# Layer 2's values and 12 of its 16 gates made ahead of its attention by seven block products for eight, by way of DRAM

## The chip, the cores and the metric

One core of one Trainium2 chip runs the kernel. The metric is the device time of one launch in microseconds (us), where a lower number is better. Five engines work beside each other, each through its own instructions in order: TensorE (PE in the profile; its weight loads are PEld), VectorE (DVE), ScalarE (ACT), GpSimd (POOL), and SyncE (SP), which issues all of this kernel's DMA transfers.

## The reference, cut to what matters

One step of a two-layer encoder over T = 576 tokens (512 of a prompt, 64 of a running stream), model width 2048. Layer 1 mixes stick-breaking attention and a state-space branch, projects, and ends in a layer norm. Layer 2 is what the change touches:

```python
def odd_layer(x, past_k, past_v, w_in, rel_bias, w_out, ln_g, ln_b):
    proj = jnp.einsum('bld,de->ble', x, w_in)          # 2048 -> 4 * 2048
    q, k, v, g = jnp.split(proj, 4, axis=-1)           # 32 heads of 64
    o = chunk_band_attention(q, k, v, past_k, past_v, rel_bias) * jax.nn.silu(g)
    mix = jnp.einsum('ble,ed->bld', o, w_out)
    return layer_norm(DEEPNORM_ALPHA * x + mix, ln_g, ln_b)
```

All is float32. The keys and values of layer 2 are outputs too.

## The kernel before

Activations lie feature-major: a feature tile is 128 features (partitions) by 576 tokens, and the model has 16 of them. Every float32 operand is split into a high and a low part of the type fp32r (`split`, L79: ACT makes the high part at L84, DVE the low part at L85), and each product of tiles is three matmuls: high weights with high data, high with low, low with high. `product` (L100) makes one output tile: two weight tiles of 128 x 1024 are fetched (`fetch`, L88, SP) and split, and then 16 feature tiles x 3 terms x 2 halves of 288 tokens = 96 matmuls run into one PSUM tile `pj` of two (`terms`, L115; the matmul is L123). The two halves follow each other on the same weights, except with `seq=True`, where the whole first half of the tokens goes ahead of the second. Raw weight tiles have two buffers, their split parts three.

Layer 1 ends in `mix_norm` (L633): the output projection, then, with no product left that could run, the normalisation tile by tile (POOL L741, DVE L742, ACT L746 and L748, DVE L749), which leaves the split activations `yh`, `yl` in SBUF and the sum of them in DRAM (`y_scr`, L751). The first two products of layer 2 (`first`, L761: the queries and the keys of head pair 0) run over the tokens as these come.

Layer 2 then goes over 16 head pairs (`run_pairs`, L505). For a pair `heads_in` (L420) makes queries, keys and values, three products, and turns the values token-major; then comes the pair's gate, a fourth product with its SiLU (`silu`, L126: four ACT and two DVE operations); then `ca_attend` (L780): logits, softmax, transposes and the weighted sum of values, gated in `place` (L527) and stored to `o_scr1`. The last four pairs leave their gate for after the loop (`ndefer` = 4), so that products run beneath the end of the last attention. The output projection and layer norm (`mix_norm`, L847) read `o_scr1` back.

Nothing here sets the order of the engines' instructions by hand: a scheduler with its own model of times takes the operations of all stages and lays them out on each engine, so products stand between the attention's small matmuls. Each engine then runs its own list in that order. So what the diff writes in one place may stand in several on the engines, and rows of that order are shown with the change.

Of the kernel before, what the change touches and what calls it, by code (L numbers as in the profile page):

```python
# [46 lines left out]
def encoder(ctx: ExitStack, tc: tile.TileContext, a):  # L47
# [78 lines left out]
    def silu(pl, src, dst, n, tag):  # L126
        """dst = src * sigmoid(src), sigmoid through exp(min(x, 0) - log(1 + exp(-|x|)))."""
        t = pl.tile([P, 580], F32, tag=tag, name=tag, bufs=2)[:, :n]
# [5 lines left out]
        tt(dst, src, t, ALU.mult)  # L134
# [38 lines left out]
    # ------------------------------------------------------------------ SSD branch  # L173
# [72 lines left out]
    SMP = 515               # column of the first sample token in a conv output  # L246
    for g in range(NG):
# [3 lines left out]
        # token-major x * dt, x * to_end, and B  # L251
# [9 lines left out]
        # masked (C B^T)^T  # L261
# [10 lines left out]
        # states  # L272
# [29 lines left out]
        # sample tokens of the whole group  # L302
# [26 lines left out]
        for i in range(4):  # L329
# [4 lines left out]
            # y of two heads  # L334
# [60 lines left out]
    def qk_sample(dst, qb, kh, kl):  # L395
        """dst [128 (2 heads x 64 queries), keys] = q . k from the block-diagonal parts of q."""
# [17 lines left out]
    def back(ap):  # L414
        """The view with its last free dim reversed."""
# [4 lines left out]
    def heads_in(pe, pl, w, mq, mk, mv, okd, ovd, pr, tiles, flipq=False, ready=None):  # L420
# [4 lines left out]
        pq = ready[0] if ready else product(w, mq, 2, xh, xl)  # L425
# [10 lines left out]
        pk = ready[1] if ready else product(w, mk, 2, xh, xl)  # L436
# [31 lines left out]
    def transpose_tile(wsrc, r, t, wts, flipq=False):  # L468
        """wsrc [128 queries of tile t of head r, keys] -> wts[block][:, head, queries of t]."""
# [26 lines left out]
    def sample_pv(blocks):  # L496
        """blocks: (w^T [keys, 128 (2 heads x 64 queries)], v [keys, 128]) -> PSUM [128, 64 queries]."""
# [29 lines left out]
    def place(pl, gt, po, get_sample, flipq=False):  # L527
        """Gated (or raw) head-pair output, feature-major [128, T]."""
# [14 lines left out]
    # ------------------------------------------------------------------ stick-breaking heads  # L543
# [411 lines left out]
```

## Time and profile before

| what | value |
|---|---|
| median of 3 runs (lowest to highest) | 2737.45 us (2735.05 to 2740.14) |
| span of the profiled execution | 2731.6 us |
| what lies between that span and the median | 5.85 us |
| instructions | 47,350 |
| PE busy | 2680.1 us, 98% |
| DVE busy | 1530.9 us, 56% |
| ACT busy | 1155.0 us, 42% |
| DMA, mean over the span | 110 GB/s |

The profile is of one execution. No time other than its span is recorded for that execution itself; the median of the runs stands in for it, 5.85 us above the span. Busy shares are averages over stages that differ, so the stages have to be read apart. Matmuls overlap in the pipeline, so a matmul's own duration (about 0.3 us) is not what it costs: the distance from the start of one to the start of the next is.

### The profile page before, as it was taken

Reading aid. Unit: us, or ns where it says so; the run is one execution under the profiler, and the core shown is the slowest. Engines: PE = TensorE matmul, PEld = TensorE weight load, DVE = VectorE, ACT = ScalarE, POOL = GpSimd, SP = SyncE. Lnnn points to the kernel's source line nnn. Section 1 sums busy time; section 2 is a strip of 40 time slices with the busy share of each in tenths; the row PEclk is TensorE's granted clock in tenths of the full one; section 3 lists DMA queues with packets and bytes.
Section 4 is the critical chain, followed back from the end, with each engine's and each line's share of the span. In section 5 each row is a group of like instructions: output and inputs, shape, how many; then the busy total and the mean of one; then the engine's idle time right before and its main releaser. Section 6 shows DMA issues by size and latency. Waiting matters only on the chain.

```text
span 2731.6 us, 47350 instructions
## 1 busy us (share of the span) xinstructions
PE 2680.1 (98%) x20126; PEld 2577.3 (94%) x20126; DVE 1530.9 (56%) x2328; ACT 1155.0 (42%) x1938; POOL 94.1 (3%) x172
## 2 busy tenths in 40 slices
PE   9999999999999999999998999999999999999996
PEld 8999899999999999999998999999999999999995
DVE  6665657665656767653338545444445555554437
ACT  5434344434555656541225434333334343344224
POOL 0000000000000000000004000000000000000004
PEclk9999999999999999999999999999999999999998
DMA  5222222223232222353235433333333333334334
GB/s 188 78 84 85 66 95 68 93 79 107 91 103 99 92 93 83 109 189 99 95 111 173 142 104 116 110 110 114 114 109 115 109 113 118 114 111 156 104 103 140
DMA packets 111060, 299.33 MB, mean 110 GB/s; under 512 B 12672, under 2 KB 26752, under 8 KB 110848
## 3 DMA queue, kind: packets, MB, share of 16 engines
q1 hardware_dynamic: 110848, 296.30, 32.8%
q8 instruction: 158, 2.59, 0.4%
q14 instruction: 54, 0.44, 0.0%
HBM read 250.82 MB, written 45.42 MB: 108 GB/s over the span
## 4 chain that ended last, share of the span: by engine, by line
PE 95%; DVE 3%; ACT 1%; issue 0%; DMA 0%; SPq 0%; ACTq 0%; DVEq 0%
PE pj L123 79%; PE po L493 3%; PE tpw L473 2%; PE px L123 2%; DVE d L742 1%; PE z L393 1%; PE z L392 1%; PE pos L502 1%; PE z L398 1%; PE pst L287 1%; PE py L356 1%; PE py L358 0%; PE tpw L485 0%; PE tpv L452 0%; PE pcb L338 0%
## 5 line engine op out<-in xcount | busy, mean ns | idle before, releaser
L85 DVE TENSOR_TENSOR wl<-raw,wh 128x1024 fp32r<-128x1024 f32 x367 | 450.6, 1228 | 490.3 <-ACT wh L84 488.3
L84 ACT ACTIVATE wh<-raw 128x1024 fp32r<-128x1024 f32 x367 | 388.3, 1058 | 739.7 <-PE pj L123 632.9
L123 PE MATMUL pj<-yl,wh 128*128 128x288 f32 x2048 | 464.4, 300 | 6.8 <-DVE yl L749 6.8
L123 PE MATMUL pj<-yh,wl 128*128 128x288 f32 x2048 | 455.2, 299 | 0.0
L123 PE MATMUL pj<-yh,wh 128*128 128x288 f32 x2048 | 451.8, 298 | 1.1 <-DVE kf L438 0.9
L123 PEld LDWEIGHTS pj<-yl,wh 128*128 128x128 f32 x2048 | 336.2, 189 | 10.8 <-DVE yl L749 9.0
L123 PEld LDWEIGHTS pj<-yh,wl 128*128 128x128 f32 x2048 | 333.3, 189 | 13.7 <-issue 12.2
L123 PEld LDWEIGHTS pj<-yh,wh 128*128 128x128 f32 x2048 | 336.0, 189 | 5.1 <-issue 2.0
L123 PE MATMUL pj<-oh,wl 128*128 128x288 f32 (+2 forms) x1120 | 254.7, 297 | 3.2 <-DVE wl L85 3.2
L123 PE MATMUL pj<-ol,wh 128*128 128x288 f32 (+2 forms) x1120 | 254.9, 297 | 0.0
L123 PE MATMUL pj<-oh,wh 128*128 128x288 f32 (+2 forms) x1120 | 254.3, 297 | 0.0
L123 PEld LDWEIGHTS pj<-oh,wl 128*128 128x128 f32 x1120 | 186.3, 189 | 3.9 <-DVE wl L85 3.4
L123 PEld LDWEIGHTS pj<-oh,wh 128*128 128x128 f32 x1120 | 186.1, 189 | 0.5
L123 PEld LDWEIGHTS pj<-ol,wh 128*128 128x128 f32 x1120 | 185.8, 189 | 0.3
L741 POOL TENSOR_TENSOR d<-d,mu 128x288 f32<-128x288 f32 (+2 forms) x60 | 60.2, 1038 | 1996.4 <-DVE mu L727 1211.3
L808 ACT ACTIVATE t<-t,smx 128x128 f32<-128x128 f32 (+3 forms) x128 | 71.1, 556 | 83.0 <-DVE smx L806 53.7
L466 ACT ACTIVATE wts<-tpw 128x128 f32<-128x128 f32 (+1 forms) x96 | 41.5, 432 | 127.2 <-PE tpw L473 127.0
L833 DVE TENSOR_TENSOR t<-z,bp 128x128 f32<-128x128 f32 (+3 forms) x128 | 60.5, 485 | 49.8 <-PE tpw L473 46.0
L493 PE MATMUL po<-wts,vt 128*64 128x384 f32 (+3 forms) x384 | 82.6, 442 | 0.0
L464 DVE COPY wts<-tpw 128x128 f32<-128x128 f32 (+1 forms) x96 | 46.7, 487 | 49.7 <-PE tpw L473 48.7
L676 DVE TENSOR_TENSOR d<-xr,pj 128x576 f32<-128x576 f32 (+3 forms) x30 | 20.2, 672 | 88.3 <-PE pj L123 88.3
L453 ACT ACTIVATE vt<-tpv 128x512 f32<-128x512 f32 x24 | 14.2, 594 | 126.4 <-PE tpv L452 126.4
(433 smaller groups left out, 5509.2 us busy)
## 6 DMA issues: line engine op xcount, KB each, us to landing
raw<-w_in SPq DMA_DIRECT2D x272, 512.0 KB, 3.3
raw<-w_out SPq DMA_DIRECT2D x95, 512.0 KB, 3.2
xr<-xT SPq DMA_DIRECT2D x29, 288.0 KB, 5.9
o_scr<-of SPq DMA_DIRECT2D x24, 288.0 KB, 3.0
d<-o_scr SPq DMA_DIRECT2D x24, 288.0 KB, 5.8
o_scr<-z SPq DMA_DIRECT2D x16, 288.0 KB, 2.2
or<-o_scr SPq DMA_DIRECT2D x16, 288.0 KB, 3.3
y_scr<-d SPq DMA_DIRECT2D x16, 288.0 KB, 3.9
```

The lines of the kernel that those rows point to most:

```text
L84: act(hi, src, AF.Copy)
L85: tt(lo, src, hi.bitcast(F32), ALU.subtract)
L123: mm(ps[:, at.start + v.start:at.start + v.stop], st[:, c], mv[u * 8 + k][:, v], start=(first and k == 0 and i == 0), stop=(last and k == ...
L287: mm(pst, btok[0:n, c, :], xe[0:n], start=True, stop=True)
L356: mm(o, xdt[:, c, hc], w4[:, r, c, :], start=True, stop=(c == 0))
L464: nc.vector.tensor_copy(dst, src)
L466: act(dst, src, AF.Copy)
L473: nc.tensor.transpose(tp[:, b * P:(b + 1) * P], wsrc[:, b * P:(b + 1) * P], ident)
L493: mm(po[q, b * P:TP], vt[:, b, q], wts[:, b, r, b * P:TP], start=(b == 0), stop=(b == 3))
L741: (tt if tail and m in (0, 1, 2, 3) else nc.gpsimd.tensor_tensor)(r, r, mu[:, v], ALU.subtract)
L808: act(t[:, i, :], t[:, i, :], AF.Exp, bias=sm[:, i:i + 1], accum_out=sm[:, 2 + i:3 + i])
L833: tt(tv[:, i, :], z[:, i * n:i * n + n], bp[seg[i][0]][:, TP - n:TP], ALU.add)
```

## The change

For two output tiles at once, one of the values and one of the gates (the last time two of the values), the 16 feature tiles are taken as two blocks of 8, the 576 tokens as two halves and the two outputs as two rows: a 2 x 2 by 2 x 2 block product. It is made by Strassen's scheme in Winograd's form, with seven block products of 8 feature tiles x 3 terms = 24 matmuls of 288 tokens (`seven`, L163; the matmul is L179), where two plain products take eight. It needs sums of weight blocks, four DVE operations of 128 x 1024 for each seven (L192, L195, L200, L203), and sums of blocks of the activations, made once (`sums_of`, L144): `y_scr` is loaded back in pairs of feature tiles, DVE makes four sums of 288 tokens of each pair (L152 to L155), and two tiles of sums are split (`ta`, `tb`). Results leave PSUM by four ACT copies and three DVE additions per seven.

Ahead of the attention there are now: two plain products with `seq=True` for the values of pairs 14 and 15 (`first`, L844), and 13 sevens, 12 for value and gate of pairs 0 to 11 and one for the values of pairs 12 and 13. Values go to a new DRAM tile `v_scr` and to the output `o_cav`, gates after their SiLU to `g_scr`. The attention loads both (L522, L592) where it had made them. Queries, keys, and the four last gates stay plain products. The pools of the sevens use the memory that `mix_norm` had before and the attention has behind them.

```diff
+    def sums_of(pl, tmp, src):
+        b12, b14 = [], []
+        for k in range(8):
+            ya, yb = (tmp.tile([P, T], F32, tag="so", name="so", bufs=4) for _ in range(2))
+            load(ya, src[k])
+            load(yb, src[8 + k])
+            tt(ya[:, 0:HALF], ya[:, HALF:T], ya[:, 0:HALF], ALU.subtract)
+            tt(ya[:, HALF:T], yb[:, HALF:T], ya[:, HALF:T], ALU.subtract)
+            tt(yb[:, HALF:T], yb[:, HALF:T], ya[:, 0:HALF], ALU.subtract)
+            tt(yb[:, 0:HALF], yb[:, 0:HALF], yb[:, HALF:T], ALU.subtract)
+            b12.append(split(pl, ya, [P, T], f"ta{k}"))
+            b14.append(split(pl, yb, [P, T], f"tb{k}"))
...
+    def seven(w, m0, m1, sums, ps, tmp):
...
+            for k in range(8):
+                c = slice(k * P, (k + 1) * P)
+                hi, lo = b[k]
+                for i, (st, mv) in enumerate(((wh, hi), (wh, lo), (wl, hi))):
+                    mm(acc, st[:, c], mv[:, v], start=(first and k == 0 and i == 0),
+                       stop=(k == 7 and i == 2), skip_group_check=not first)
+
+        a11, a21, a22 = raw(m0, 0, "sr", tmp, 4), raw(m1, 0, "sr", tmp, 4), raw(m1, 1, "sr", tmp, 4)
+        s_ = raw(None, 0, "raw", wpool, 2)
+        a12 = raw(m0, 1, "raw", wpool, 2)
...
+        mul(pa, "M1", a11, True)
+        act(c11, pa, AF.Copy)
+        tt(s_, a21, a22, ALU.add)
+        mul(pc, "M5", s_, True)
+        act(c22, pc, AF.Copy)
+        tt(s_, s_, a11, ALU.subtract)
+        mul(pa, "M6", s_, False)
+        act(c12, pa, AF.Copy)
+        mul(pb, "M2", a12, True)
+        tt(c11, c11, pb, ALU.add)
+        tt(a21, a11, a21, ALU.subtract)
+        mul(pa, "M7", a21, False)
+        tt(c22, c22, pa, ALU.add)
+        tt(s_, a12, s_, ALU.subtract)
+        mul(pc, "M3", s_, False)
+        tt(c12, c12, pc, ALU.add)
+        mul(pa, "M4", a22, False)
+        act(c21, pa, AF.Copy)
...
-        pv = product(w, mv, 2, xh, xl)
         vf = pe.tile([P, T], F32, tag="kvf", name="vf", bufs=2)
-        nc.vector.tensor_copy(vf, pv)
-        store(ovd[pr], vf)
+        if mv is None:
+            load(vf, ovd[pr])
...
-                pg = product(wg, gate0 + pr, 2, xh, xl)
                 gt = lt.tile([P, T], F32, tag="gt", name="gt", bufs=1)
-                silu(lt, pg, gt, T, "st")
+                if gates is None:
+                    silu(lt, product(wg, gate0 + pr, 2, xh, xl), gt, T, "st")
+                else:
+                    load(gt, gates[pr])
...
-    first = [product(a["w_in1"], m, 2, xh, xl, seq=True) for m in (0, 16)]
+    NSEV = 12
+    ps7 = pool("ps7", bufs=1, space=PSUM)
+    first = [product(a["w_in1"], 32 + m, 2, xh, xl, seq=True) for m in (14, 15)]
+    tp7 = pool("t7", bufs=1, side="left")
+    tm7 = pool("tm7", bufs=1, side="left")
+    for m, pv in zip((14, 15), first):
+        vf = tm7.tile([P, T], F32, tag="so", name="so", bufs=4)
+        nc.vector.tensor_copy(vf, pv)
+        store(v_scr[m], vf)
+        store(a["o_cav"][m], vf)
+    sums = sums_of(tp7, tm7, y_scr)
+    for i in range(NSEV + 1):
+        pair = (i, i) if i < NSEV else (12, 13)
+        o0, o1 = seven(a["w_in1"], 32 + pair[0], (48 if i < NSEV else 32) + pair[1], sums, ps7, tm7)
+        store(v_scr[pair[0]], o0)
+        store(a["o_cav"][pair[0]], o0)
+        if i < NSEV:
+            silu(tm7, o1, o1, T, "st7", 1)
+            store(g_scr[i], o1)
+        else:
+            store(v_scr[pair[1]], o1)
+            store(a["o_cav"][pair[1]], o1)
```

**Where the first products of layer 2 end, on PE.** Before, the second sequential product (its last rows read `yh15`) was followed by the next product of the attention (`pj_15394`), whose data all lie in SBUF:

```order
L123 MATMUL pj_15232<-yh15_14926,wl_15242 128x288
...
L123 MATMUL pj_15394<-yh0_14911,wh_15397 128x288 x2
L123 MATMUL pj_15394<-yl0_14927,wh_15397 128x288 x2
L123 MATMUL pj_15394<-yh0_14911,wl_15398 128x288 x2
```

Now the first seven stands there: M1 into `pa`, one matmul of M5 on the first sum `ta0h`, then M2 (`pb`), then the rest of M5 and M6 on the sums of each k in turn:

```order
L125 MATMUL pj_15237<-yh15_14928,wl_15247 128x288
L179 MATMUL pa_15497<-yh0_14913,wh_15502 128x288
...
L179 MATMUL pb_15498<-yl8_14937,wh_15591 128x288
L179 MATMUL pc_15499<-ta0h_15368,wh_15532 128x288
L179 MATMUL pb_15498<-yh8_14921,wl_15592 128x288
...
L179 MATMUL pb_15498<-yh15_14928,wl_15592 128x288
L179 MATMUL pc_15499<-ta0l_15369,wh_15532 128x288
...
L179 MATMUL pc_15499<-ta7h_15480,wl_15533 128x288
L179 MATMUL pa_15497<-tb7h_15484,wh_15562 128x288
...
L179 MATMUL pc_15499<-yh8_14921,wh_15651 128x288
```

So PE comes to data that are made at that moment; M3 (the last row), M7 and M4 stand behind all of the sums.

**The same place on DVE and SP.** DVE's list, behind the last `yl` of the layer norm (L829 in the new numbering): copies of the plain values, the sums, and the low parts and sums of weights, in one row:

```order
L829 TENSOR_TENSOR yl_14944<-d,yh_14928 128x288
L849 COPY so<-pj 128x576
L87 TENSOR_TENSOR wl<-sr,wh 128x1024
L192 TENSOR_TENSOR raw<-sr 128x1024
L200 TENSOR_TENSOR sr<-sr 128x1024
L849 COPY so<-pj 128x576
L87 TENSOR_TENSOR wl<-raw,wh 128x1024
L152 TENSOR_TENSOR so<-so 128x288
L195 TENSOR_TENSOR raw<-raw,sr 128x1024
...
L87 TENSOR_TENSOR wl<-raw,wh 128x1024 x2
L87 TENSOR_TENSOR ta0l<-so,ta0h 128x576
L203 TENSOR_TENSOR raw<-raw 128x1024
```

SP's list at that place, the loads of weights, stores and loads of `y_scr` behind its last stores:

```order
L831 DMA y_scr<-d 128x2x288 x8
L168 DMA sr<-w_in 128x1024 x4
L850 DMA v_scr<-so 128x576
L851 DMA o_cav<-so 128x576
L150 DMA so<-y_scr 128x576
L151 DMA so<-y_scr 128x576
L150 DMA so<-y_scr 128x576
L850 DMA v_scr<-so 128x576
```

Before, the eighth of these stores had only weight loads and the attention's own small loads behind it; now the loads of the new stage, whose buffers lie where the layer norm's tiles were, come behind it.

**Where the last attention ends, on PE.** Before, a whole gate product (`pj_25408`) stood between the last pair's weighted sums (`po_25028`, `pos_25039`) and the output projection (`pj_25634`):

```order
L502 MATMUL pos_25039<-wss_24899,cv_24895 64x64 x8
L502 MATMUL pos_25039<-wss_24899,vt_24872 64x64 x2
...
L123 MATMUL pj_25408<-yh0_14911,wh_25411 128x288 x2
...
L123 MATMUL pj_25408<-yh15_14926,wl_25466 128x288 x2
L123 MATMUL pj_25634<-oh0_25543,wh_25639 128x288 x2
```

Now the gates are all done by then, part of the output projection (`pj_25860`) stands ahead of the last pair, and its third tile `px_25861` right behind:

```order
L125 MATMUL pj_25860<-oh2_25778,wl_25919 128x288 x2
L551 MATMUL tpw_25217<-cst_67,t_25208 128x128 x4
...
L571 MATMUL po_25253<-wts_25123,vt_25097 64x512 x2
...
L580 MATMUL pos_25264<-wss_25124,vt_25097 64x64 x2
L125 MATMUL px_25861<-oh0_25768,wh_25972 128x288 x2
```

The gate products moved ahead into the attention of the last pairs.

## Rows read from the trace of the kernel before

**Rows 1.** The page: engines' busy time, and the chain of waits by engine and line
```profile
PE 2680.1 (98%) x20126; PEld 2577.3 (94%) x20126; DVE 1530.9 (56%) x2328; ACT 1155.0 (42%) x1938; POOL 94.1 (3%) x172
...
PE 95%; DVE 3%; ACT 1%; issue 0%; DMA 0%; SPq 0%; ACTq 0%; DVEq 0%
```

**Rows 2.** Windows: stretch, length, busy PE PEld DVE ACT POOL, clock, DMA share, GB/s
```profile
1622.30:1684.60 62.30, 62.30 (x473) 59.94 (x472) 30.86 (x60) 24.10 (x47) 0.00 (x0) 1.00 0.36 115
500.00:600.00 100.00, 100.00 (x734) 97.28 (x733) 62.20 (x79) 44.81 (x65) 6.28 (x20) 1.00 0.27 92
700.00:800.00 100.00, 98.54 (x743) 94.45 (x742) 68.18 (x107) 59.96 (x105) 0.00 (x0) 1.00 0.27 92
800.00:900.00 100.00, 99.82 (x780) 94.74 (x779) 56.34 (x89) 49.84 (x87) 0.00 (x0) 1.00 0.29 95
900.00:1000.00 100.00, 97.57 (x758) 91.97 (x757) 68.34 (x107) 61.95 (x111) 0.00 (x0) 1.00 0.30 100
1000.00:1100.00 100.00, 98.21 (x758) 92.28 (x758) 70.23 (x109) 60.55 (x108) 0.00 (x0) 1.00 0.25 83
```

**Rows 3.** Timeline of PE in a plain product: start, length, line, count
```profile
1300.21 0.43 PE L123 MATMUL pj<-oh,wh 128*128 128x288 f32 x2
...
1302.61 0.42 PE L123 MATMUL pj<-oh,wh 128*128 128x288 f32 x2
```

**Rows 4.** Timeline of PE where halves go one at a time
```profile
1440.06 0.30 PE L123 MATMUL px<-oh,wh 128*128 128x288 f32 x1
...
1442.69 0.30 PE L123 MATMUL pj<-oh,wl 128*128 128x288 f32 x1
```

**Rows 5.** Timeline of PE where the attention takes over from the first products
```profile
1523.14 0.50 PE L123 MATMUL pj<-yh,wh 128*128 128x288 f32 x2 [0.94 <-DVE kf L438]
```

**Rows 6.** Timeline of SP: the 16 loads of layer 1's projection; last store of y_scr
```profile
1171.86 10.09 SPq L649 DMA_DIRECT2D d<-o_scr  x16
...
1511.60 0.36 SPq L751 DMA_DIRECT2D y_scr<-d  x1
```

**Rows 7.** DMA issues of the page: count, size each, us to landing
```profile
y_scr<-d SPq DMA_DIRECT2D x16, 288.0 KB, 3.9
...
xr<-y_scr SPq DMA_DIRECT2D x13, 288.0 KB, 2.9
```

**Rows 8.** Timeline of ACT: the split of the last of these 16 loads
```profile
1188.49 0.69 ACT L650 ACTIVATE oh<-d 128x576 fp32r<-128x576 f32 x1 [0.99 <-DMA d<-o_scr]
```

**Rows 9.** Timeline of DVE: back to back low parts of 288 and of 576 tokens
```profile
1511.93 1.20 DVE L749 TENSOR_TENSOR yl<-d,yh 128x288 fp32r<-128x288 f32 x3 [0.40 <-ACT yh L748]
...
2482.39 1.43 DVE L651 TENSOR_TENSOR ol<-or,oh 128x576 fp32r<-128x576 f32 x2 [0.87 <-ACT oh L650]
```

**Rows 10.** Groups of instructions on DVE within one head pair of layer 2
```profile
L85 DVE TENSOR_TENSOR wl<-raw,wh 128x1024 fp32r<-128x1024 f32 x8 | 9.8, 1222 | 11.8 <-ACT wh L84 11.7
...
L447 DVE COPY vf<-pj 128x576 f32<-128x576 f32 x1 | 0.8, 759 | 4.6 <-PE pj L123 4.6
...
L134 DVE TENSOR_TENSOR gt<-pj,st 128x576 f32<-128x576 f32 x1 | 0.7, 749 | 0.0
L132 DVE SCALAR_TENSOR_TENSOR st<-pj,st 128x576 f32<-128x576 f32 x1 | 0.7, 747 | 0.0
```

**Rows 11.** Groups of instructions on ACT in the same head pair
```profile
L84 ACT ACTIVATE wh<-raw 128x1024 fp32r<-128x1024 f32 x8 | 8.5, 1058 | 11.1 <-PE pj L123 5.7 <-issue 5.4
```

**Rows 12.** Windows behind layer 1's layer norm (columns as in rows 2)
```profile
1498.00:1510.00 12.00, 8.02 (x28) 6.58 (x28) 11.89 (x21) 8.63 (x18) 8.98 (x14) 0.50 0.27 98
...
1512.00:1514.00 2.00, 2.00 (x18) 2.00 (x17) 1.13 (x3) 0.57 (x2) 0.00 (x0) 1.00 0.86 251
```

**Rows 13.** Timeline of PE there: the first dense matmuls, and the first fast ones
```profile
1506.37 0.61 PE L123 MATMUL pj<-yl,wh 128*128 128x288 f32 x1
...
1511.06 0.30 PE L123 MATMUL pj<-yh,wh 128*128 128x288 f32 x1
```

**Rows 14.** Timeline of PE: the last pair's sums, and the projection's first matmul
```profile
2481.18 0.33 PE L502 MATMUL pos<-wss,vt 64*64 64x64 f32 x4
...
2495.01 0.43 PE L123 MATMUL pj<-oh,wh 128*128 128x288 f32 x2
```

More of the change, by code (lines that the diff above doesn't have):

```diff
@@ L77, in encoder @@
     y_scr = dram.tile([NK, P, T], F32, name="y_scr")
+    v_scr = dram.tile([NPAIR_CA, P, T], F32, name="v_scr")
+    g_scr = dram.tile([NPAIR_CA, P, T], F32, name="g_scr")
     def split(pl, src, shape, tag, bufs=None):
@@ L124, in terms, with silu @@
                        start=(first and k == 0 and i == 0), stop=(last and k == 7 and i == 2))
-    def silu(pl, src, dst, n, tag):
-        t = pl.tile([P, 580], F32, tag=tag, name=tag, bufs=2)[:, :n]
+    def silu(pl, src, dst, n, tag, bufs=2):
+        t = pl.tile([P, 580], F32, tag=tag, name=tag, bufs=bufs)[:, :n]
         act(t, src, AF.Abs)
@@ L134, in silu @@
         tt(dst, src, t, ALU.mult)
+    def sums_of(pl, tmp, src):
[10 more added lines that the diff above has]
+            b14.append(split(pl, yb, [P, T], f"tb{k}"))
+        lo_, hi_ = slice(0, HALF), slice(HALF, T)
+        x1, x2 = [(xh[k], xl[k]) for k in range(8)], [(xh[8 + k], xl[8 + k]) for k in range(8)]
+        return {"M1": (x1, lo_), "M2": (x2, lo_), "M3": (x2, hi_), "M5": (b12, lo_), "M7": (b12, hi_),
+                "M4": (b14, lo_), "M6": (b14, hi_)}
@@ new lines, in seven, with raw, mul @@
+    def seven(w, m0, m1, sums, ps, tmp):
+        def raw(m, u, tag, pl, bufs):
+            t = pl.tile([P, 1024], F32, tag=tag, name=tag, bufs=bufs)
+            if m is not None:
+                load(t, w[m, u])
+            return t
+        def mul(acc, which, wt, first):
+            wh, wl = split(wpool, wt, [P, 1024], "w")
+            b, v = sums[which]
+            for k in range(8):
[7 more added lines that the diff above has]
+        a12 = raw(m0, 1, "raw", wpool, 2)
+        pa = ps.tile([P, 512], F32, tag="pa", name="pa", bufs=2)[:, 0:HALF]
+        pb = ps.tile([P, 512], F32, tag="pb", name="pb", bufs=1)[:, 0:HALF]
+        pc = ps.tile([P, 512], F32, tag="pc", name="pc", bufs=1)[:, 0:HALF]
+        o0, o1 = (tmp.tile([P, T], F32, tag="so", name="so", bufs=4) for _ in range(2))
+        c11, c12, c21, c22 = o0[:, 0:HALF], o0[:, HALF:T], o1[:, 0:HALF], o1[:, HALF:T]
+        mul(pa, "M1", a11, True)
[16 more added lines that the diff above has]
+        act(c21, pa, AF.Copy)
+        return o0, o1
@@ L418, in back, with heads_in @@
                        ap=[list(x) for x in ap.ap[:-1]] + [[-st, n]])
-    def heads_in(pe, pl, w, mq, mk, mv, okd, ovd, pr, tiles, flipq=False, ready=None):
+    def heads_in(pe, pl, w, mq, mk, mv, okd, ovd, pr, tiles, flipq=False):
         keys, qb = tiles
         turn = back if flipq else (lambda x: x)
-        pq = ready[0] if ready else product(w, mq, 2, xh, xl)
+        pq = product(w, mq, 2, xh, xl)
         qs = []
@@ L435, in heads_in @@
         qbs = split(pl, qb, [P, P], "qb")
-        pk = ready[1] if ready else product(w, mk, 2, xh, xl)
+        pk = product(w, mk, 2, xh, xl)
         kf = pe.tile([P, T], F32, tag="kvf", name="kf", bufs=2)
@@ L444, in heads_in @@
             tt(kl[r][q], kf[q, 0:TP], kh[r].bitcast(F32)[q], ALU.subtract)
-        pv = product(w, mv, 2, xh, xl)
         vf = pe.tile([P, T], F32, tag="kvf", name="vf", bufs=2)
-        nc.vector.tensor_copy(vf, pv)
-        store(ovd[pr], vf)
+        if mv is None:
+            load(vf, ovd[pr])
+        else:
+            pv = product(w, mv, 2, xh, xl)
+            nc.vector.tensor_copy(vf, pv)
+            store(ovd[pr], vf)
         vt = pl.tile([P, 5, P], F32, tag="vt", name="vt", bufs=2)
@@ L503, in sample_pv, with run_pairs @@
         return po[:, 0:TS]
-    def run_pairs(lt, npair, ndefer, heads, attend, wg, gate0, scr):
+    def run_pairs(lt, npair, ndefer, heads, attend, wg, gate0, scr, gates=None):
         pend = []
@@ L758, in encoder @@
     xp, xh, xl = mix_norm(24, o_scr0, a["w_out0"], a["xT"], V_G0, V_B0, HALF, y_scr, True)
-    first = [product(a["w_in1"], m, 2, xh, xl, seq=True) for m in (0, 16)]
+    NSEV = 12
[5 more added lines that the diff above has]
+        vf = tm7.tile([P, T], F32, tag="so", name="so", bufs=4)
+        nc.vector.tensor_copy(vf, pv)
+        store(v_scr[m], vf)
[9 more added lines that the diff above has]
+            store(g_scr[i], o1)
+        else:
+            store(v_scr[pair[1]], o1)
+            store(a["o_cav"][pair[1]], o1)
+    tm7.release()
+    tp7.release()
+    ps7.release()
     pm = pool("pmc", bufs=1, space=PSUM)
@@ L776, in ca_heads @@
     def ca_heads(pr):
-        return heads_in(ce_, c_, a["w_in1"], pr, 16 + pr, 32 + pr, a["o_cak"], a["o_cav"], pr, ca_tiles, True,
-                        None if pr else first)
+        return heads_in(ce_, c_, a["w_in1"], pr, 16 + pr, None, a["o_cak"], v_scr, pr, ca_tiles, True)
     def ca_attend(pr, st, gt):
@@ L838, in ca_attend @@
             [(wss[:, b, :], cv[:, b, :]) for b in range(4)] + [(wss[0:TS, 4, :], vt[0:TS, 4, :])]), True)
-    run_pairs(cl_, NPAIR_CA, 4, ca_heads, ca_attend, a["w_in1"], 48, o_scr1)
+    run_pairs(cl_, NPAIR_CA, NPAIR_CA - NSEV, ca_heads, ca_attend, a["w_in1"], 48, o_scr1, g_scr)
     cl_.release()
```

## The prediction

> **What bounds the kernel now.** First the page's busy times and its chain of waits [rows 1]: PE is busy 2680.1 of 2731.6 us, and 95% of the chain that ended last is PE. The reader should see that PE's own work is the time; DVE at 56% is an average. Then the windows [rows 2], stage by stage: a head pair of layer 2 takes 62.30 us in which PE never stops, with DVE busy 30.86 us and ACT 24.10. So beneath layer 2's attention nothing on DVE, ACT or DMA costs anything at present, and one matmul less is its whole pitch less. The rows of layer 1's stages in the same view tell what happens with a busier DVE: at 62% (500 to 600) PE still loses nothing, in the stick-breaking stage (700 to 1100, DVE 56 to 70%) it loses 1.46 + 0.18 + 2.43 + 1.79 = 5.86 us of 400, 1.5%. Last the place where layer 1 goes over into layer 2, since the change puts a new dependent stage there. About 0.2% (5.5 us) is what a measurement of this kernel can tell from no change.
>
> **The change, part by part.** The sum is made against the profiled execution, span 2731.6 us; the median of the runs is 5.85 us above it, and I carry that offset over.
>
> 1. *Matmuls.* Layer 2 had 64 products of 96 matmuls; now 16 for queries, 16 for keys, 2 for values and 4 for gates are left, so 26 are removed: 26 x 96 = 2,496. In a product two matmuls share their weights: from 1300.21 to 1302.61 there are 9 rows of two, 18 matmuls, 2.40/18 = 0.1333 us each [rows 3]; 332.8 us go. Added are 13 sevens x 7 x 24 = 2,184 matmuls, each with weights of its own. The nearest rows run one half at a time: 20 steps from 1440.06 to 1442.69, 0.1315 us each [rows 4]; 287.2 us come. Net **-45.6** (-41.6 if they take the product's 0.1333). New weights at each matmul so cost no more than every second one. The Trainium skill (TensorE: Matmul & The Clock Gate, section Back-to-back issue gap) gives N/2.4 + 2.5 ns for one matmul alone, 122.5 ns at 288 columns, by which the 312 matmuls saved would be worth 38.2 us and not 45.6, and the whole sum below would be +1.4 instead of -6.0. The trace does not agree with 122.5 at either spacing, and the measured rows decide.
>
> 2. *Removed beside them:* the 0.94 us that PE waited for the copy of the first keys [rows 5]: **-0.9**. Removed DVE and ACT work was hidden (PE full in the pair's row).
>
> 3. *Start of the sevens.* The two plain products in front take the place of two equal ones: these ended at 1522.2, 0.94 us ahead of the row at 1523.14 [rows 5]. The tiles of the new stage lie where the layer norm's were, so on SP its loads start behind the last store of `y_scr`, issued at 1511.60 [rows 6] and landed some 3.9 us later [rows 7]: 1515.5. Ahead of the first sum stand four weight tiles, two stores and two loads, 4 x 0.524 + 4 x 0.295 = 3.28 MB. Sixteen loads of 0.295 MB, issued from 1171.86 [rows 6], were there at 1188.49 [rows 8]: 284 GB/s, so 11.5 us, and the first pair of `y_scr` tiles is there at 1527.0. Each of 8 k steps then costs DVE four sums (1.20/3 = 0.40 us each) and two low parts (1.43/2 = 0.72) [rows 9], 3.0 us: 24.0. In the same queue stand 7 operations on weights of 1.22 us [rows 10]: 8.5. A chain of load (2.9 us [rows 7]), sums, high and low parts must free its buffer before the k step after next can load, for which I add 4.5 us of gaps (0 to 9). The last sum is split at 1564. PE does M1, M2 and, k by k, M5 and M6 meanwhile; M3, M7 and M4 are left, 72 x 0.1315 = 9.5 us. It comes to them at half clock: behind the layer norm PE was 8.02 of 12 us busy at a granted 0.50 (1.2 GHz of 2.4) [rows 12], and its first 18 dense matmuls took from 1506.37 to 1511.06, 4.69 us [rows 13] for 2.37 at the fast pitch: 2.4 us. With 0.5 for the hand-over from DVE the first seven ends at 1576.4, 54.2 us after 1522.2, for 22.1 us of work (168 x 0.1315). **+32** (17 to 39). The low end has the transfers at once and DVE's chain shared with the weights' half; the high one has each load exposed.
>
> 4. *Steady sevens.* 22.1 us of PE each. DVE: 7 low parts and 4 sums of weights (11 x 1.22 = 13.4), 3 additions of 0.40, two SiLU operations of 0.75 [rows 10]: 16.1 us, 73%. ACT: 7 x 1.06 [rows 11] and less than 5 us of copies and SiLU, 55%. No row has PE beside DVE at 73%; the nearest lose 0 at 62% and 1.8 to 2.4% at 68 to 70% [rows 2]. A block's weights may be made while the two blocks ahead of it run (three buffers), 6.3 us for an operation of 1.22. So I take **+2** for the 12 sevens, bounds 0 and 7 (2.4% of 287).
>
> 5. *Seam into the attention.* Its memory is free when the last seven ends; queries and keys of pair 0, 192 matmuls or 25 us, read only `yh` and `yl` and cover its first loads. **+1** (0 to 3).
>
> 6. *Attention with two products.* A pair's PE time falls to 62.3 - 192 x 0.1333 = 36.7 us; DVE's to 30.86 - 4 x 1.22 - 0.76 - 1.50 = 23.7 [rows 2, 10], 65%. Between the row with 62% and none, and the stage with 66% and 1.5% lost: 0 to 9 us of 16 x 36.7 = 587, I take **+3.5**. The loads of values and gates stand on SP ahead of weight loads; a gate's buffer is single, so its load waits for the pair before to be placed, just behind that pair's store, which waited for the same before.
>
> 7. *Tail.* From the last pair's sums at 2481.18 to the projection at 2495.01 there were 13.8 us of gate product [rows 14], under which the last outputs went to DRAM and back. Now some 14 us of the projection's first weight half stand there instead; a store and a load of 3 us each [rows 7] with the copies fit. **+2** (0 to 5).
>
> Sum: -45.6 - 0.9 + 32 + 2 + 1 + 3.5 + 2 = **-6.0**: span 2725.6, time 2737.45 - 6.0 = **2731.4 us**.
>
> **The rivals.**
>
> *A, slower: DVE's queue sets the pace of the sevens.* Everything DVE does stands in one queue: if an addition that waits for PSUM, or a SiLU step that waits for ACT, stands ahead of the next low part, PE gets it late in each seven. For it: 73% busy, more than any stage that keeps PE full. Against it: two blocks of lead. It decides from (6.0 + 2 + 5.5)/13 = 1.04 us per seven. At one low part late by its own 1.22 us it gives -8 + 15.9 = +7.9: 2745; at 1.75 us, 2752. Attention pairs that lose 1 us each (16 for 3.5) give +6.5, 2744, by the same kind of queue.
>
> *B, faster: the start is short.* If the sums' loads come with no gap, and of the weights' work only M1's, M5's and M6's (two sums, three low parts, 6.1 us) stand ahead of the last sum, this is ready at 1527.0 + 24.0 + 6.1 = 1557, the first seven ends at 1569.5, and the start costs 25.2: -12.8, 2724.6; with the attention at no loss, 2721. For it: SP has little else to move there. Against it: order of DVE's rows, in which M2's low part and M7's and M3's sums stand among the k steps as well.
>
> *C, no net change:* Strassen saves its 45.6 and the start takes 39, its high end: +1 in all, 2738. That the scheduler undoes the change is excluded by the order of instructions: the 2,184 matmuls stand there.
>
> **How the numbers follow.** My sum with its smaller errors, 2724 to 2738 around 2731: 0.52, about half of it below -5.5 us. A: 0.21. B: 0.15. C: 0.12, a quarter of it above +5.5 as its neighbours are. Faster by over 0.2%: 0.52 x 0.55 + 0.15 = 0.44; slower: 0.21 x 0.85 + 0.12 x 0.25 = 0.21; the same: 0.35. The range leaves out the far half of B and the last third of A: 2718 to 2751.
>
> **What would show it.** Matmuls 312 fewer, 0.131 us apart in the sevens; a stretch of about 40 us behind 1525 in which PE is a third busy at half clock, waiting for the low parts of `ta` and `tb`; then sevens 22 to 22.5 us apart; pairs 37 us apart; hardly a wait at the projection. I am wrong if the sevens stand over 23 us apart, if PE is dense before 1555, or if the last sum comes after 1572.

## The result, and the profile after

The changed kernel takes 2750.66 us (median of 4 runs, 2749.05 to 2755.56), the kernel before 2736.84 us (4 runs); the ratio is 1.0055, 95% interval 1.0041 to 1.0069. It is slower by 13.8 us where I forecast faster by 6.0.

The page of the changed kernel, its busy times and its chain of waits, answers to [rows 1]:

```profile
PE 2667.3 (97%) x19814; PEld 2551.4 (93%) x19814; DVE 1670.5 (61%) x2492; ACT 1224.1 (44%) x2045; POOL 94.1 (3%) x172
...
PE 91%; DVE 4%; DMA 2%; ACT 2%; issue 1%; SPq 0%; ACTq 0%; DVEq 0%
```

PE has its 312 matmuls fewer, and yet its share of the chain fell from 95% to 91%: waits on DVE, ACT and DMA came in. Where they are is told by the windows of the changed kernel (columns as in [rows 2]): the first seven, a steady one, the pair with the longest waits, a steady pair, and the end of the attention.

```profile
1529.10:1582.80 53.70, 33.70 (x170) 29.24 (x169) 42.38 (x67) 19.71 (x27) 0.00 (x0) 0.71 0.51 163
1582.80:1605.10 22.30, 22.30 (x170) 22.30 (x169) 15.94 (x17) 11.22 (x15) 0.00 (x0) 1.00 0.41 134
2141.00:2179.00 38.00, 36.89 (x276) 33.97 (x276) 24.14 (x52) 17.33 (x39) 0.00 (x0) 1.00 0.43 135
2256.10:2294.10 38.00, 37.36 (x281) 34.44 (x280) 24.08 (x52) 17.35 (x40) 0.00 (x0) 1.00 0.43 135
2500.00:2540.00 40.00, 33.63 (x221) 30.13 (x220) 19.62 (x28) 17.12 (x29) 0.00 (x0) 0.87 0.45 150
```

The steady seven has PE full although DVE is busy 15.94 of 22.30 us. The first takes 53.7 us, of which PE works 33.7, and at a clock of 0.71. Seven pairs in a row start 38.0 us apart; PE is idle 0.64 us in each of these and 1.1 us in the costliest. At the end 6.4 of 40 us are idle and the clock is 0.87.

One thing before the sizes. The profiled execution of the change is the slowest of its four runs, and its span, 2753.8 us, stands 22.2 us above that of before, not 13.8. Part of this lies in layer 1, whose instructions stand in the same order in both kernels: on DVE the last three low parts of the layer norm start at 1518.82 us, those of before at 1511.93 [rows 9].

```profile
1518.82 1.19 DVE L829 TENSOR_TENSOR yl<-d,yh 128x288 fp32r<-128x288 f32 x3 [0.39 <-ACT yh L828]
```

So 6.9 us belong to the execution and 15.3 us to layer 2. The timeline of PE in the changed kernel shows the three places. The start:

```profile
1529.24 0.30 PE L179 MATMUL pa<-yh,wh 128*128 128x288 f32 x1
...
1538.50 0.61 PE L179 MATMUL pb<-yh,wh 128*128 128x288 f32 x1 [5.89 <-ACT wh L86]
...
1572.09 0.40 PE L179 MATMUL pc<-yh,wh 128*128 128x288 f32 x1 [0.92 <-ACT so L194]
...
1582.96 0.29 PE L179 MATMUL pa<-yh,wh 128*128 128x288 f32 x1
...
1605.24 0.29 PE L179 MATMUL pa<-yh,wh 128*128 128x288 f32 x1
```

The first row is the first matmul of the first seven, the last two those of the second and third: 53.72 us for the first, 22.28 for the next. Between, M2's weights come 5.89 us late, then M5 and M6 go step by step, and M3 starts at 1572.09. The pair with the longest waits, on PE, and what DVE and ACT do in that time:

```profile
2141.65 0.60 PE L530 MATMUL tpv<-cst,vf 128*128 128x128 f32 x4
2142.09 0.27 PE L551 MATMUL tpw<-cst,t 128*128 128x128 f32 x1
2143.14 0.33 PE L551 MATMUL tpw<-cst,t 128*128 128x128 f32 x1 [0.78 <-DVE wts L542]
2143.80 0.30 PE L533 MATMUL tpv<-cst,vf 128*64 128x128 f32 x1 [0.33 <-ACT vt L531]
2144.04 0.54 PE L125 MATMUL pj<-yh,wh 128*128 128x288 f32 x2
```

```profile
2142.07 0.69 DVE L506 SCALAR_TENSOR_TENSOR q<-pj,q 64x512 fp32r<-64x512 f32 x1 [0.94 <-ACT q L505]
2142.80 0.29 DVE L542 COPY wts<-tpw 128x128 f32<-128x128 f32 x1
...
2142.07 1.06 ACT L86 ACTIVATE wh<-raw 128x1024 fp32r<-128x1024 f32 x1
2143.14 0.60 ACT L531 ACTIVATE vt<-tpv 128x512 f32<-128x512 f32 x1
```

Transposes stand in a row with no product matmul between them. The next group needs the PSUM tile (each of the two, `tpw` and `tpv`, has one buffer) that DVE or ACT has still to copy out: 0.78 + 0.33 us here, 0.38 + 0.26 in a steady pair. The copies are short, 0.29 and 0.60 us; in these rows they come late because a step for the queries (DVE) and a split of weights (ACT) stand ahead of them. All such waits of PE from 1850 to 2560 us, the attention (total us, times, longest):

```profile
PE tpw L551 <- DVE wts L542: 5.0, 11, 0.8
PE tpv L533 <- ACT vt L531: 3.7, 10, 0.8
```

So not every one of the 16 pairs waits. The end:

```profile
2502.87 0.44 PE L551 MATMUL tpw<-cst,t 128*128 128x128 f32 x2 [0.52 <-DVE wts L542]
2503.78 0.66 PE L551 MATMUL tpw<-cst,t 128*128 128x128 f32 x4 [0.47 <-ACT wts L544]
2505.80 0.85 PE L125 MATMUL pj<-oh,wh 128*128 128x288 f32 x2 [1.36 <-DVE gt L136]
...
2512.03 0.55 PE L551 MATMUL tpw<-cst,t 128*128 128x128 f32 x3 [0.69 <-ACT wts L544]
2513.23 0.55 PE L551 MATMUL tpw<-cst,t 128*128 128x128 f32 x3 [0.65 <-DVE wts L542]
...
2532.01 1.00 PE L125 MATMUL pj<-oh,wh 128*128 128x288 f32 x4 [2.34 <-ACT oh L730]
```

The last pair waits at four of its transposes, a product matmul 1.36 us for `gt` from DVE, and the projection then 2.34 us for outputs that went through DRAM. The longer matmuls behind 2505.80 and 2532.01 are at half clock (0.50 in the column before the DMA share):

```profile
2505.20:2511.90 6.70, 5.54 (x22) 5.13 (x22) 1.63 (x4) 1.15 (x3) 0.00 (x0) 0.50 0.02 7
2532.50:2535.80 3.30, 3.30 (x16) 3.30 (x15) 2.29 (x4) 2.59 (x4) 0.00 (x0) 0.50 0.25 97
```

### The profile page after: what moved, and what is told of

It is laid out like the page before. It is cut to its first block, busy times and chain, and to the rows that moved or that the text cites. A ratio compares the mean times of both kernels' runs of the same rounds, so it can differ in the third digit from the quotient of the medians.

```text
span 2753.8 us, 47284 instructions
## 1 busy us (share of the span) xinstructions
PE 2667.3 (97%) x19814; PEld 2551.4 (93%) x19814; DVE 1670.5 (61%) x2492; ACT 1224.1 (44%) x2045; POOL 94.1 (3%) x172
## 4 chain that ended last, share of the span: by engine, by line
PE 91%; DVE 4%; DMA 2%; ACT 2%; issue 1%; SPq 0%; ACTq 0%; DVEq 0%
PE pj L125 66%; PE pa L179 6%; PE pc L179 3%; PE po L571 3%; PE tpw L551 2%; PE px L125 2%; PE pb L179 1%; DVE d L822 1%; PE z L466 1%; PE z L467 1%; PE pos L580 1%; ACT wh L86 1%; PE z L472 1%; DVE wl L87 1%; PE pst L361 1%
## 5 line engine op out<-in xcount | busy, mean ns | idle before, releaser
L125 PE MATMUL pj<-yl,wh 128*128 128x288 f32 x1216 | 275.5, 300 | 6.2 <-DVE yl L829 6.1
L125 PE MATMUL pj<-yh,wl 128*128 128x288 f32 x1216 | 278.2, 300 | 0.0
L125 PE MATMUL pj<-yh,wh 128*128 128x288 f32 x1216 | 275.5, 300 | 2.5 <-DVE kf L513 1.4
L125 PEld LDWEIGHTS pj<-yl,wh 128*128 128x128 f32 x1216 | 201.2, 190 | 9.4 <-DVE yl L829 8.5
L125 PEld LDWEIGHTS pj<-yh,wh 128*128 128x128 f32 x1216 | 201.1, 190 | 7.3 <-DVE kf L513 3.3
L125 PEld LDWEIGHTS pj<-yh,wl 128*128 128x128 f32 x1216 | 202.9, 190 | 2.5 <-DVE wl L87 0.2
L571 PE MATMUL po<-wts,vt 128*64 128x512 f32 (+3 forms) x384 | 82.1, 442 | 0.0
L86 ACT ACTIVATE wh<-sr 128x1024 fp32r<-128x1024 f32 x39 | 41.4, 1061 | 59.0 <-PE pa L179 32.2
```

The costliest lines, as they stand in the source:

```text
L86: act(hi, src, AF.Copy)
L125: mm(ps[:, at.start + v.start:at.start + v.stop], st[:, c], mv[u * 8 + k][:, v], start=(first and k == 0 and i == 0), stop=(last and k == ...
L571: mm(po[q, b * P:TP], vt[:, b, q], wts[:, b, r, b * P:TP], start=(b == 0), stop=(b == 3))
```

## The experiments

The theory was formed on these rows: three separate losses, at the start (31 us), in the pairs (some 13 us in all) and at the end (10 us), against 13 x (25.6 - 22.3) = 43 us saved. The first four runs tell them apart.

**The new order without Strassen.**

```diff
-    sums = sums_of(tp7, tm7, y_scr)
...
-        o0, o1 = seven(a["w_in1"], 32 + pair[0], (48 if i < NSEV else 32) + pair[1], sums, ps7, tm7)
+        o0, o1 = (tm7.tile([P, T], F32, tag="so", name="so", bufs=4) for _ in range(2))
+        nc.vector.tensor_copy(o0, product(a["w_in1"], 32 + pair[0], 2, xh, xl))
+        p1 = product(a["w_in1"], (48 if i < NSEV else 32) + pair[1], 2, xh, xl)
...
```

> The same order of the work as the change, with values and gates made ahead and sent through DRAM, but by plain products: no sums, no sevens. Theory (the change loses at three places: about 31 us at the start of the sevens, about 13 us in an attention with two products a pair, about 10 us at the last pair, against 43 us that 13 sevens save at 25.6 - 22.3 us each): the start's loss and the saving go, the other two stay: 2737 + 13 + 10 = 2760, with pairs again 38 us apart and the last pair's waits again there. Rival (the loss belongs to the sevens and their traffic, the new order is harmless): 2737, pairs 36.7 us apart.

Measured: 2753.96 us against 2736.35 for the kernel before, ratio 1.0071 (1.0055 to 1.0088). Its windows, of a pair, at the end, and where the sevens started:

```profile
2140.00:2178.00 38.00, 36.89 (x277) 33.97 (x277) 24.03 (x52) 17.26 (x40) 0.00 (x0) 1.00 0.41 135
2500.00:2540.00 40.00, 34.55 (x257) 31.16 (x257) 19.91 (x30) 18.49 (x29) 0.00 (x0) 1.00 0.51 171
1529.00:1580.00 51.00, 51.00 (x385) 51.00 (x383) 14.16 (x15) 13.86 (x16) 0.00 (x0) 1.00 0.35 125
```

The pair loses what it loses in the change, the end nearly as much idle time (5.45 us for 6.37) but no half clock, and nothing is lost where the sevens started. So making the values and gates ahead costs 17.6 us by itself (23 had been expected). All of Strassen, its start included, is then worth 2754.0 - 2750.7 = 3.3 us, which the runs do not tell from nothing: the intervals of the two ratios overlap. The profiles give a second measure, layer 2 alone, from the last matmul of its first two products to one and the same matmul of the output projection (kernel before, this run, change):

```profile
1521.90 0.29 PE L123 MATMUL pj<-yh,wl 128*128 128x288 f32 x1
2542.89 0.43 PE L123 MATMUL pj<-oh,wl 128*128 128x288 f32 x2
```

```profile
1521.20 0.29 PE L125 MATMUL pj<-yh,wl 128*128 128x288 f32 x1
2563.39 0.43 PE L125 MATMUL pj<-oh,wl 128*128 128x288 f32 x2
```

```profile
1529.11 0.29 PE L125 MATMUL pj<-yh,wl 128*128 128x288 f32 x1
2564.72 0.43 PE L125 MATMUL pj<-oh,wl 128*128 128x288 f32 x2
```

These are 1021.0, 1042.2 and 1035.6 us: by one execution of each, the new order costs 21.2 us and Strassen brings 6.6 back, or some 10 without the half clock at the change's end (about 4 us, an estimate worked out further below). This stretch is called the length of layer 2 from here on.

**Cover for the start.**

```diff
-    for i in range(NSEV + 1):
+    for m in (12, 13):
+        pv = product(a["w_in1"], 32 + m, 2, xh, xl)
+        vf = tm7.tile([P, 580], F32, tag="st7", name="st7", bufs=1)[:, :T]
+        nc.vector.tensor_copy(vf, pv)
...
+    for i in range(NSEV):
```

(These lines stand ahead of the sums.)

> The values of pairs 12 and 13 by two plain products ahead of the first seven, not by the thirteenth seven. Theory (PE waits at the start for sums that need nothing of PE, so products hide them): 25.6 us of cover for 3.3 us of saving given up; 20 to 26 us come back: 2750.7 + 3.3 - 23 = 2731, and PE's idle time between the last value product and the second seven falls from 18 us to under 5. Rival (the sums are held up by loads and by a DVE queue that the products' own weights lengthen): the start is put off by as much as it is covered, 2745 to 2752.

Measured: 2730.89 us, ratio 0.9979 (0.9968 to 0.9990): 20 us better than the change, as expected, and faster than before. In its profile the first seven takes 33.4 us where the change's takes 53.7, so 20 us of the start are back and 11 are still lost; PE is idle 6.1 us there, a little more than the 5 that the theory allowed.

**The values of the last four pairs back in the attention.**

```diff
-    first = [product(a["w_in1"], 32 + m, 2, xh, xl, seq=True) for m in (14, 15)]
+    first = [product(a["w_in1"], m, 2, xh, xl, seq=True) for m in (0, 16)]
...
-        return heads_in(ce_, c_, a["w_in1"], pr, 16 + pr, None, a["o_cak"], v_scr, pr, ca_tiles, True)
+        own = pr >= NSEV
+        return heads_in(ce_, c_, a["w_in1"], pr, 16 + pr, 32 + pr if own else None, a["o_cak"],
+                        a["o_cav"] if own else v_scr, pr, ca_tiles, True, None if pr else first)
...
```

(The lines not shown drop the copies and stores of the two values and the thirteenth seven, and hand `first` to pair 0.)

> Pairs 12 to 15 make their values in the attention as before, the two products under the layer norm are again pair 0's queries and keys and stay in PSUM, and there are 12 sevens. Theory (the end lost its time because the last pairs had too few products left): the last pair's waits and the half clock there go, -10; four pairs lose nothing any more, -4; no copies of values hold the buffers of the sums, -3 at the start; one seven fewer, +3.3: 2737. Rival (the end's wait comes from reading the outputs back, whatever stands beside): 2748 to 2754, with the wait for the last feature tiles of the projection still there.

Measured: 2738.70 us, ratio 1.0010 (0.9998 to 1.0022). Its window at the end:

```profile
2500.00:2540.00 40.00, 40.00 (x303) 40.00 (x302) 18.98 (x23) 15.72 (x21) 0.00 (x0) 1.00 0.55 186
```

No idle time and no half clock here: the end had lost its cover, and reading the outputs back is hidden as soon as products stand beside it. A loss of the same kind stands at another place now: behind the last seven comes pair 0, whose queries and keys are already made, and PE is idle 4.3 us there, between 1828 and 1859 us, with 3.4 us at half clock from 1857.7 on.

**What sets the pace of the start.**

```diff
-            tt(ya[:, 0:HALF], ya[:, HALF:T], ya[:, 0:HALF], ALU.subtract)
-            tt(ya[:, HALF:T], yb[:, HALF:T], ya[:, HALF:T], ALU.subtract)
-            tt(yb[:, HALF:T], yb[:, HALF:T], ya[:, 0:HALF], ALU.subtract)
-            tt(yb[:, 0:HALF], yb[:, 0:HALF], yb[:, HALF:T], ALU.subtract)
```

> Leaves out the four DVE sums of each of the 8 steps at the start (the loaded tiles are split as they are), so values and gates are not what they should be. Theory (DVE's queue sets the pace of the start: 3.0 us of 3.9 us a step): 8 x 1.6 = 12.8 us of DVE go, the start is 9 to 12 us shorter: 2740. Rival (the loads in their four buffers set it): less than 4 us, 2747 to 2751.

Measured: 2739.87 us, 10.8 us less than the change. The window over its first seven, where 32 DVE operations are missing:

```profile
1526.10:1569.80 43.70, 31.87 (x170) 27.88 (x169) 30.38 (x35) 20.00 (x27) 0.00 (x0) 0.77 0.59 202
```

43.7 us instead of 53.7, for 12.0 us less work on DVE (42.38 to 30.38 us busy): DVE's queue sets the pace of the start, and part of what is left is not DVE's work (30.4 of 43.7 us busy). In the change itself DVE waits eight times for loads of `y_scr`, 4.3 us in all.

The next four build on that.

**Both cover and end.** Against the run with the last values back: `first` makes value and gate of pair 11, two more products value and gate of pair 10, ten sevens follow.

```diff
...
+    keep(11, *first)
+    sums = sums_of(tp7, tm7, y_scr)
+    keep(10, *[product(a["w_in1"], m, 2, xh, xl) for m in (32 + 10, 48 + 10)])
+    for i in range(NSEV - NPL):
```

(`keep` copies or gates the two results and stores them.)

> Ten sevens (value and gate of pairs 0 to 9); value and gate of pair 11 plain under the layer norm, of pair 10 plain as cover of the start; pairs 12 to 15 make their values in the attention and their gates behind it as before. Theory (three separate losses: start, pairs with two products, end): against the run with four plain values, two sevens fewer +6.6, no loss at the last pair -7, four more pairs without loss -5, start shorter by 0 to 5: 2731 - 8 = 2723. Rival (the end and the pairs lose for another reason): 2731 + 6.6 = 2738.

Measured: 2729.51 us, ratio 0.9974 (0.9965 to 0.9983). This lies between the two forecasts. By the profiles, against four plain values, attention and end gave back 10.7 us (the four products that came back into them counted at 12.8 us each), the two sevens given up took 6.6 of it, and the first seven became 2.6 us longer (36.0 for 33.4), although the sums are written first; why the start grew is open.

**Six plain products ahead.**

```diff
-    for i in range(NSEV + 1):
+    for m in (12, 13, 11):
+        pv = product(a["w_in1"], 32 + m, 2, xh, xl)
...
+    pv = product(a["w_in1"], 48 + 11, 2, xh, xl)
...
+    for i in range(NSEV - 1):
```

> Six plain products ahead (values of pairs 11 to 15, gate of pair 11) and eleven sevens, the sums written ahead of the added products. Theory (cover is all that the start lacks): the 11 us that the first two sevens still lost with four plain products go, one seven fewer is +3.3: 2731 - 8 = 2723, the first seven 22.3 to 24 us. Rival (the products' weights push the sums back in DVE's and SP's queues): the first two sevens lose as much as with four, 2734.

Measured: 2720.28 us, ratio 0.9942 (0.9925 to 0.9959). Its window from the first seven on has no idle PE:

```profile
1574.00:1619.00 45.00, 45.00 (x341) 44.95 (x340) 30.64 (x32) 22.05 (x29) 0.00 (x0) 1.00 0.38 126
```

The first seven takes 22.4 us. With 51 us of cover (four products of 12.8) the start costs nothing.

**Only values ahead, three products a pair.**

```diff
-        o0, o1 = seven(a["w_in1"], 32 + pair[0], (48 if i < NSEV else 32) + pair[1], sums, ps7, tm7)
+        o0, o1 = seven(a["w_in1"], 32 + pair[0], 32 + pair[1], sums, ps7, tm7)
...
-    run_pairs(cl_, NPAIR_CA, NPAIR_CA - NSEV, ca_heads, ca_attend, a["w_in1"], 48, o_scr1, g_scr)
+    run_pairs(cl_, NPAIR_CA, NPAIR_CA - NSEV, ca_heads, ca_attend, a["w_in1"], 48, o_scr1)
```

(with four plain values ahead and six sevens.)

> Only values are made ahead: four plain (pairs 12 to 15) and six sevens of two values each; the gates stay in the attention, so a pair has three products. Theory (a pair with two products has too few matmuls between its transposes): pairs are 11.1 + 3 x 12.8 = 49.5 us apart and lose nothing; 6 x 3.3 = 20 us saved, 11 lost at the start, 1 at the seam: 2736.4 - 8 = 2728. Rival (a pair loses 1.3 us because its values come from DRAM, whatever is beside): pairs 50.8 us apart, 2744.

Measured: 2731.80 us, ratio 0.9982 (0.9973 to 0.9992). Two pairs in a window:

```profile
2035.00:2134.00 99.00, 99.00 (x751) 94.34 (x751) 55.96 (x111) 43.24 (x90) 0.00 (x0) 1.00 0.37 119
```

49.5 us a pair, PE full, although the values come from DRAM here too. That is also the distance of the kernel before where its last pairs have three products, 49.55 us. So the pair's loss is one of cover: two products are too few, three are enough. The time is 4 us above the forecast of 2728, which had nothing for the last pair and the projection; PE is idle 3.8 us there in this profile too.

**Two PSUM banks for the transposes**, on the run with four plain values:

```diff
-        tp = pm.tile([P, 512], F32, tag="t", name="tpw")
+        tp = pm.tile([P, 512], F32, tag="t", name="tpw", bufs=nt[0])
...
-            z = pm.tile([P, 512], F32, tag="s", name="z", bufs=2)
+            z = pm.tile([P, 512], F32, tag="s", name="z", bufs=1)
```

(`nt[0]` is 2 in layer 2 and 1 ahead of it. The other tiles of the same tag, `tpn` and `pos`, change likewise; the transposes of values, `tpv`, keep their one buffer.)

> The run with four plain values, but in layer 2's attention the transposes have two PSUM banks in turn and the logits one (before: one and two). Theory (PE waits because the next transposes need the bank that ACT or DVE is still emptying): pairs 36.7 to 37.3 us apart for 38.0, 2731 - 13 = 2718. Rival (the chain of the softmax is too long for the cover, whatever the banks; or the logits wait now): pairs 38 us or more apart, 2731 to 2745.

Measured: 2720.46 us, ratio 0.9946 (0.9931 to 0.9961), 10.4 us less than with one bank. Three pairs, and all waits of PE from the sevens' end on:

```profile
2033.00:2146.00 113.00, 111.48 (x839) 103.38 (x838) 75.40 (x154) 52.26 (x119) 0.00 (x0) 1.00 0.44 136
```

```profile
PE pj L125 <- DVE kf L515: 8.1, 10, 1.4
```

No wait at a transpose is left. But this edit changed two things: with two banks the scheduler also laid out the pairs anew (three steps of 42.3, 35.1 and 35.5 us in turn), and products now stand between the transposes in PE's list. The waits at `tpv`, whose buffers were not changed, went with the others. So that PE waited for the bank is told by its rows in the change; this run does not separate the bank from the order. And a pair is 113/3 = 37.7 us, not 36.7 to 37.3: a wait for the keys' copy has come in its place, 0.8 us a time. Most of the gain lies at the end, where the last pair has no waits now.

The last four put the parts together by the edits shown above, and the banks where they should not matter.

> Six plain products ahead and two banks for the transposes together. Theory (start and attention are separate losses): both gains stand beside each other, 2720.3 - 10.4 = 2710. Rival (both moved the same wait): 2717 to 2721.

Measured: 2713.23 us, ratio 0.9914 (0.9900 to 0.9929): 7 us better than six plain products alone and the fastest of all; most of the two gains add up. In the lengths of layer 2 they add up wholly: the banks take 8.3 us off with four plain values (1013.81 to 1005.55) and 9.3 with six products (1006.93 to 997.68).

> The change itself with two PSUM banks for the transposes and one for the logits in layer 2's attention, nothing else. Theory (pairs and the end of the attention lose to the one bank, whatever stands ahead): 10 to 13 us come back, the half clock at the last pair with them: 2739. Rival (the banks helped only beside the shorter start): 2748.

Measured: 2738.51 us, ratio 1.0004 (0.9995 to 1.0014): the banks, with the order that comes with them, bring the change back to the time before. The half clock at the end is gone too, as expected.

> Five plain products ahead (values of pairs 12 to 15, gate of pair 12), twelve sevens, three gates left for the end, two banks for the transposes. Theory (cover counts, 38.4 us for a start that lost 31): the start loses 0 to 3, one seven more than with six: 2710 - 3 + 2 = 2709. Rival (the end needs its fourth gate): its last pair waits again, 2714 or more.

Measured: 2714.58 us, ratio 0.9920 (0.9905 to 0.9935). Its start, 34 us from the first seven's first matmul on:

```profile
1561.00:1595.00 34.00, 30.17 (x217) 28.77 (x216) 27.18 (x38) 15.40 (x23) 0.00 (x0) 1.00 0.41 132
```

3.8 us are still idle at the start and the first seven takes 27.7 us, 5.4 more than a steady one, which takes up what the seven that it has more saves. The rival's number came out, but not for its reason: behind the last pair's transposes PE has no idle time in this run nor in the one with six, so three gates at the end were enough.

> The kernel before with two banks for the transposes and one for the logits in layer 2's attention. Theory (PE loses nothing there with three and four products a pair, so there is nothing to win): 2736, pairs 62.3 us apart. Rival (the banks help in any case): 2726.

Measured: 2741.06 us, ratio 1.0017 (1.0008 to 1.0026). Two pairs:

```profile
1622.00:1747.50 125.50, 125.50 (x945) 119.95 (x944) 63.61 (x117) 48.77 (x95) 0.00 (x0) 1.00 0.34 111
```

62.7 us a pair with PE full, for 62.3 before: where nothing waits, the banks win nothing, and lose 0.4 us a pair, whose cause I did not look for. So the 12 us that they bring in the change are its own, not a gain that was there before.

## Why the prediction was wrong

By its steps, against the profile of the change:

1. *Matmuls, -45.6:* nearly. 13 sevens of 22.29 us are 289.8 us for the 332.8 removed, -43.0; the pitch in a seven is 22.28/168 = 0.1326 us, not 0.1315 as in [rows 4]. The estimate of 0.1225 us from the formula for one matmul alone in the Trainium skill (TensorE: Matmul & The Clock Gate, section Back-to-back issue gap) is 8% below what the rows show.
2. *Removed wait, -0.9:* right; the first seven starts 0.13 us behind the last product's matmul.
3. *Start, +32:* right, 53.72 - 22.29 = +31.4, and by the mechanism named: taking away 12.0 us of DVE's sums shortened it by 10. The last low part of the sums ends 41.0 us behind the two products, forecast 41.8, and DVE's waits for loads, 4.3 us, are the 4.5 us of gaps that I had added. One term was not spent: PE came to M3 at full clock (1.00 from 1570 to 1580), not at half.
4. *Steady sevens, +2:* 0. The sevens are 22.28 to 22.29 us apart with PE full beside a DVE at 71%. So rival A's main mechanism was wrong, as was its condition: a DVE busier than in any stage of [rows 2] did not hold up PE. That the two blocks of lead are the reason was not tested. (The rows at 68 to 70% lost 1.5 to 2.4%, not 1.8 to 2.4 as I wrote.)
5. *Seam, +1:* 0, no idle time is shown there.
6. *Attention, +3.5, bounds 0 and 9:* **this step failed first.** A steady pair takes 38.0 us and not 36.7. An estimate for all: the 15 steps from the first pair's transposes to the last one's, at 36.7 us each and 0.1333 us for every product matmul that stands there besides, come to 16.6 us less than they took. The second and third step lose nothing; the scheduler had put half a product more into them. Only 9.1 us of this are idle time in the profile. The rest stands beside the waits in rows that count as busy: a lone transpose is listed with 0.27 us, while in a row of four they start 0.11 us apart. I had scaled by DVE's busy share and taken layer 1's stages as the measure; DVE's share came out at 63%, near the 65% forecast, and told nothing of the loss. What counted was how many product matmuls stand between one transpose and the next that needs its PSUM tile: none at the place shown, and with three products a pair lost nothing. Only the aside in rival A, that pairs lose 1 us each, had the size; it gave +6.5, 2744. Its place was half right: PE waits for copies that stand in DVE's and in ACT's queue, and it could wait only because no product was there to run meanwhile.
7. *End, +2, bounds 0 and 5:* **this failed too.** I counted the path from the last pair's sums to the projection and found 14 us of cover. It lost before these sums as well: the last pairs' own transposes had no gate products left beside them, since these had been drawn forward. Its idle time is 6.4 us and the half clock comes on top, some 11 us with the seam (27.8 below, less the 16.6 of step 6); with the last values back, or with two banks and their order, the idle time and the half clock there are gone.

The sum: -43.0 - 0.9 + 31.4 = -12.5 where I had -14.5 (start included), and 27.8 us instead of 8.5 for sevens, seam, attention and end, with 6.9 us that the profiled execution had lost before layer 2. The price of the cover taken away was not in the sum at its true size. C, no net change, had a dearer start than the real one and the same small attention, so its +1 was too small for the same reason. The range reached up to 2751 only for rival A, whose sevens did not happen; that the time lies at this edge is luck.

What was left open: how much of the start, beyond DVE's 10 us, is the order in DVE's queue; whether two banks would help without the new order that came with them; and why a two-bank attention costs 0.4 us a pair where nothing waits. The share of the half clock at the end can be told from the record: behind the sevens, the run with four plain values has the same matmuls on PE in the same order, no half clock there, and is 4.8 us shorter with 0.8 us less idle time. So about 4 us of the profiled change, an estimate, are half clock, and these came with one execution: other runs in that order had 6.8, 3.4 or none at half clock there, where the change had 10.2.

## What to carry to other kernels

Work that is taken out of a stage to be made ahead is also taken away as cover: before costing it at its own duration, look which dependent steps (here transposes through one PSUM tile, and the last pair's path) it stood between, and count what stands there afterwards. A stage that needs its operands prepared wants enough independent products in front (here the start lost 31 us with none, 11 with 26 us of them, 5 with 38 and 0 with 51), even dearer ones: two sevens given up, 6.6 us, brought the 31 us of the start back. Taking away one wait (here at the transposes) can bring up the next (the keys' copy), so look at the distance of the pairs and not only at the list of waits. A kernel in the same order with the plain arithmetic tells a reordering's cost and an algorithm's gain apart.

## What the runs showed of the hardware

The clock dips of layer 1 are not the same in each execution. In the same instructions, behind each group of the state-space branch, the granted clock fell to half in some executions and not in others, and for a longer or a shorter time. Windows of the change, and then of before:

```profile
146.50:153.00 6.50, 6.50 (x29) 5.93 (x28) 3.24 (x4) 1.44 (x2) 0.00 (x0) 0.50 0.27 81
303.50:310.00 6.50, 6.50 (x30) 5.94 (x30) 3.39 (x5) 1.44 (x2) 0.00 (x0) 0.50 0.29 81
460.50:467.00 6.50, 6.50 (x30) 5.80 (x31) 3.48 (x5) 1.44 (x2) 0.00 (x0) 0.50 0.22 81
```

```profile
146.00:153.00 7.00, 7.00 (x63) 5.61 (x63) 3.91 (x5) 1.44 (x2) 0.00 (x0) 1.00 0.29 75
303.00:306.20 3.20, 3.20 (x15) 3.08 (x15) 2.02 (x3) 1.29 (x2) 0.00 (x0) 0.51 0.56 161
460.00:467.00 7.00, 7.00 (x68) 6.66 (x67) 5.48 (x9) 4.34 (x6) 0.00 (x0) 1.00 0.26 76
```

PE counts as busy in both, but 29 matmuls run in 6.5 us in one and 63 in 7.0 us in the other. At the four places (the fourth is near 618) the profiled change falls behind the kernel before by 2.9, 1.4, 2.8 and 1.3 us, matmul for matmul; it had been 1.2 us ahead. That comes to 7.2 us on PE, or the 6.9 us on DVE by which it was late before layer 2 began. Two profiles should be laid side by side from a common instruction on, not from zero.
